# Gate products of the recurrent unit as pairs of 64-row matmuls, one block of 64 channels on each half of the array

## The chip, the core and the metric

The kernel runs on one core of a Trainium2 chip. TensorE multiplies, VectorE (DVE) and ScalarE (ACT) do elementwise work, GpSimd (POOL) keeps small edge columns and issues adding transfers, and SyncE (SP) issues the other transfers. The metric is the device time of one execution in microseconds; the time of a version is the median of its runs.

## What is computed

A decoder layer on 2048 positions of 1024 channels: norm, input projection `w_in`, two mixers side by side, output projection, norm, gated feed-forward with convolutions, norm. The change concerns one mixer, a recurrent unit with 16 heads of 64 channels, whose two gates use one 64x64 matrix per head:

```python
xh = x.reshape(bsz, s, LRU_HEADS, LRU_HEAD_DIM)
r = jax.nn.sigmoid(jnp.einsum('bshi,hij->bshj', xh, wa).reshape(bsz, s, c) + ba)
i = jax.nn.sigmoid(jnp.einsum('bshi,hij->bshj', xh, wx).reshape(bsz, s, c) + bx)
log_a = -RG_C * r * jax.nn.softplus(-lam)
a = jnp.exp(log_a)
b = jnp.sqrt(-jnp.expm1(2.0 * log_a)) * (i * x)
h[t] = a[t] * h[t-1] + b[t]            # then y = h * gelu(gate)
```

`x` here is the convolved projection (the kernel's `cv`), and y goes on to the output projection.

## The kernel before

Channels lie on the 128 partitions, positions along the free dimension, in two halves of 1024 positions, each as two blocks of 512. [...]

For each half of the positions, `in_phase` goes over twelve units in the order L0 L1 S0 L2 L3 S1 L4 L5 S2 L6 L7 S3. An L unit is a block of 128 channels, two heads, of the recurrent mixer; an S unit is one of the short convolution. An input product (`in_product`, 48 matmuls into two PSUM tiles) makes each unit's operands. For an L unit `lru_conv` scales the product out of PSUM (DVE, `evac`, L371), convolves (ACT and DVE, `cv`) and splits the result into `xch` and `xcl`. `gate_weights` splits the block's gate weights into `gw`. `lru_gates` then makes the two gate products: the weights of each gate are a 128x128 matrix with the two heads' 64x64 matrices on the diagonal and zeros elsewhere, and 2 gates x 3 parts x 2 position blocks are 12 matmuls into four PSUM tiles, `zr` and `zi`. They run through `product_step` (L234), the line of the input products too. `lru_scan` follows: sigmoids (ACT, L335), exponential `a`, tanh, square, square root (L342), the scan (DVE, L346) and the multiplication by gelu (L350), which gives y. [...]

After the twelve units come the sweeps of the output projection, a seven-product scheme on blocks of positions and channels. Every sweep has three steps; each step loads a weight page and an activation page (`wr_o`) and splits both (`wh_o`, `fh_o` on ACT, `wl_o`, `fl_o` on DVE). The activation pages are y and sums of y, which go through DRAM (`y_d_B`, `y_d_T`): block 7's y is written and read back for the third step of the first sweep.

The order of the work on TensorE, SP and POOL is that of the program text (`manual_schedule`); ACT and DVE are ordered by a scheduler, by its own estimate of durations and by priorities (`tc.high_priority`: the sigmoids and the evacuations above the weight splits, these above the rest). Each engine then works strictly in its order. PSUM has eight tiles of 512 columns, taken in turn; weights have two raw buffers (`wr`) and ten pages. The gate weights lie in the raw buffer of the input block that is loaded with them, so that buffer is not free before `gw` has been split.

The last lines of the file lay out the inputs on the host, `w_gate` among them.

Of the kernel before, what the change touches and what calls it, by code (L numbers as in the profile page):

```python
# [9 lines left out]
AF = mybir.ActivationFunctionType  # L10
ALU = mybir.AluOpType

P = 128
# [3 lines left out]
T = 1024  # L17
NB = 512
NH = S // T
NLRU = 8  # L20
# [5 lines left out]
HW = 90  # L26
HE = 30
WARM = 11
NOUT = NLRU + NSC
NI = NFF // 2  # L30
NO = NOUT // 2
W_OPS = ["W21", "W11", "W22", "W12"]
# [27 lines left out]
O_BA = O_LCB + 8  # L60
O_BX = O_BA + 8
# [7 lines left out]
def block_kernel(  # L69
# [11 lines left out]
    nc = tc.nc  # L81
# [7 lines left out]
    prm = cp.tile([P, NPAR], F32, name="prm")  # L89
# [24 lines left out]
    def col(o):  # L114
        return prm[:, o : o + 1]
# [4 lines left out]
    def act(name):  # L120
        return page(name, "act", 28)

    def wpage(name):
        return page(name, "w", 10)
# [7 lines left out]
    def raw_tile(name):  # L132
        return sb.tile([P, 6, NB], F32, name=name, tag="wr", bufs=2)

    def pst(name):
        return pp.tile([P, NB], F32, name=name, tag="ps")

    def pst2(name):
        return [pst(f"{name}_b{b}") for b in range(T // NB)]

    def flat(t):
        return t.rearrange("p a b -> p (a b)")

    def r32(ap):
        return ap.bitcast(F32R)

    def blk(b):
        return slice(b * NB, (b + 1) * NB)
# [45 lines left out]
    def split(hi, lo, src):  # L194
        nc.scalar.activation(r32(hi), src, AF.Copy)  # L195
        nc.vector.tensor_tensor(r32(lo), src, hi, ALU.subtract)  # L196
# [6 lines left out]
    gate_raw = {}  # L203

    def load_parts(src, name, parts, gate=None):
        tile_ = raw_tile(f"wr_{name}")
        raw = flat(tile_)
        hi = flat(wpage(f"wh_{name}"))
        lo = flat(wpage(f"wl_{name}"))
        n = T // parts  # L210
        for i in range(parts):
            ks = slice(i * n, (i + 1) * n)
            nc.sync.dma_start(raw[:, ks], src[:, ks])
            with tc.high_priority(offset=HW):
                split(hi[:, ks], lo[:, ks], raw[:, ks])
            if gate is not None and i == 0:
                gate_raw[gate] = tile_[:, 4, : 2 * P]
                nc.sync.dma_start(gate_raw[gate], w_gate[gate])
            yield hi, lo

# [5 lines left out]
    def wcol(hl, k):  # L226
        s = slice(k * P, (k + 1) * P)
        return hl[0][:, s], hl[1][:, s]

    def product_step(ps, w, x, first, last):  # L230
        (whi, wlo), (xhi, xlo) = w, x
        for i, (a, b) in enumerate(((whi, xhi), (whi, xlo), (wlo, xhi))):
            for t in range(T // NB):
                nc.tensor.matmul(  # L234
                    ps[t], r32(a), r32(b[:, blk(t)]), start=(first and i == 0), stop=(last and i == 2)
                )
# [76 lines left out]
    def gate_weights(c, half):  # L313
        raw = gate_raw[c]
        gw = flat(act(f"gw{half}_{c}"))
        hi, lo = gw[:, 0 : 2 * P], gw[:, 2 * P : 4 * P]
        with tc.high_priority(offset=HW):
            split(hi, lo, raw)
        return hi, lo

    def lru_gates(c, half, xc, gw):
        pss = []
        for g, name in enumerate("ri"):
            ps = pst2(f"z{name}{half}_{c}")
            product_step(ps, wcol(gw, g), xc, True, True)
            pss.append(ps)
        return pss

    def lru_scan(c, half, cv, g, ps_r, ps_i):
        n = f"{half}_{c}"  # L330
        r, i, a = (flat(act(f"{x}{n}")) for x in "ria")
        with tc.high_priority(offset=HP):
            for dst, ps, o in ((r, ps_r, O_BA), (i, ps_i, O_BX)):
                for b, p in enumerate(ps):
                    nc.scalar.activation(dst[:, blk(b)], p, AF.Sigmoid, bias=col(o + c))  # L335
        nc.vector.tensor_tensor(i, i, cv, ALU.mult)
        m = cv
        nc.scalar.activation(a, r, AF.Exp, scale=nc8[:, c : c + 1])
        nc.scalar.activation(m, r, AF.Tanh, scale=c8[:, c : c + 1])
        nc.scalar.activation(r, a, AF.Square)  # L340
        nc.vector.scalar_tensor_tensor(m, r, 1.0, m, ALU.add, ALU.mult)
        nc.scalar.activation(m, m, AF.Sqrt)  # L342
        nc.vector.tensor_tensor(i, i, m, ALU.mult)
        h = r
        init = 0.0 if half == 0 else h_last[:, c : c + 1]
        nc.vector.tensor_tensor_scan(h, a, i, init, ALU.mult, ALU.add)  # L346
        if half < NH - 1:
            nc.gpsimd.tensor_copy(h_last[:, c : c + 1], h[:, T - 1 : T])
        nc.scalar.activation(g, g, AF.Gelu_apprx_tanh)
        nc.vector.tensor_tensor(h, g, h, ALU.mult)  # L350
        return h
# [60 lines left out]
    def in_phase(half, acts, acc, between):  # L412
# [29 lines left out]
        for n, (kind, c) in enumerate(UNITS):  # L442
# [22 lines left out]
            if n % 2 == 0:  # L465
                put(y_d[half], 5 if n < NOUT - 2 else 4, n // 2, "B11", y[:, blk(0)])
                even = y
# [7 lines left out]
    def put(dst, when, i, op, src):  # L475
        defer(when, dst[op][i // 2][:, i % 2, :], src)
# [265 lines left out]
    warm = pst("warm")  # L742
    for i in range(WARM):
        nc.tensor.matmul(warm[:, :P], ones, ones, start=True, stop=True)
# [172 lines left out]
def _cols(a):  # L917
    import numpy as np

    a = np.asarray(a)  # L920
    return a.reshape(-1, P).T
# [18 lines left out]
def _arrange(i):  # L940
    import numpy as np

    f = {k: np.asarray(v) for k, v in i.items()}
    x = f["x"]
    out = {}
    out["xT"] = x[0].T.reshape(KC, P, S)
    out["w_in"] = f["w_in"][0].reshape(KC, P, 28, P).transpose(2, 1, 0, 3).reshape(28, P, D)
    wg = np.zeros((NLRU, P, 2, P), x.dtype)
    for g, name in enumerate(("lru_wa", "lru_wx")):
        w = f[name][0].reshape(NLRU, 2, 64, 64)  # L950
        wg[:, 0:64, g, 0:64] = w[:, 0]
        wg[:, 64:128, g, 64:128] = w[:, 1]
    out["w_gate"] = wg.reshape(NLRU, P, 2 * P)
    w = f["w_out"][0].reshape(NOUT, P, D)
    out["w_out"] = _blocks(w[[c if kind == "L" else NLRU + c for kind, c in UNITS]], NO)
    out["w_down"] = _blocks(f["w_down"][0], NI)
    out["w_up"] = f["w_up"][0].reshape(KC, P, 2 * NFF, P).transpose(2, 1, 0, 3).reshape(2 * NFF, P, D)
    out["par"] = np.concatenate(
        [
            _cols(f["norm1_g"][0]),  # L960
            _cols(f["norm2_g"][0]),
            _cols(f["final_g"]),
            _taps(f["lru_conv_w"][0]),
            _cols(f["lru_conv_b"][0]),
            _cols(f["lru_ba"][0]),
            _cols(f["lru_bx"][0]),
            _cols(f["lru_lambda"][0]),
            _taps(f["sc_conv_w"][0]),
            _taps(f["ffn_conv_w"][0]),
        ],  # L970
        axis=1,
    )
    return {k: np.ascontiguousarray(v) for k, v in out.items()}
# [23 lines left out]
```

## Time and profile before

| | us |
|---|---|
| median of 3 runs (2310.92 to 2312.91) | 2312.73 |
| profiled execution | 2314.18 |
| its span, first to last instruction | 2312.4 |
| TensorE busy | 2278.3 |
| DVE busy | 1724.5 |
| ACT busy | 1135.9 |
| granted TensorE clock, mean | 0.993 |

The profile records one execution. A row of a timeline gives start, duration, engine, line, operation, output and inputs, shape and count, and in brackets the engine's idle time before it and what ended that. PEld rows are weight loads, SPq rows are transfers being issued. The chain of waits is followed back from the last instruction. In half 0 the twelve units take from the start to about 345 us, in half 1 from about 490 to 797 us, and the sweeps of the output projection follow each.

### The profile page before, as it was taken

Reading aid. Unit: us, or ns where it says so; the run is one execution under the profiler, and the core shown is the slowest. Engines: PE = TensorE matmul, PEld = TensorE weight load, DVE = VectorE, ACT = ScalarE, POOL = GpSimd, SP = SyncE. Lnnn points to the kernel's source line nnn. Section 1 sums busy time; section 2 is a strip of 40 time slices with the busy share of each in tenths; the row PEclk is TensorE's granted clock in tenths of the full one; section 3 lists DMA queues with packets and bytes.
Section 4 is the critical chain, followed back from the end, with each engine's and each line's share of the span. In section 5 each row is a group of like instructions: output and inputs, shape, how many; then the busy total and the mean of one; then the engine's idle time right before and its main releaser. Section 6 shows DMA issues by size and latency. Waiting matters only on the chain.

```text
span 2312.4 us, 26025 instructions
## 1 busy us (share of the span) xinstructions
PE 2278.3 (99%) x9984; PEld 1879.7 (81%) x9984; DVE 1724.5 (75%) x1910; ACT 1135.9 (49%) x1242; POOL 143.7 (6%) x232
## 2 busy tenths in 40 slices
PE   9999998999999999999999999999999999999997
PEld 7788887888888877888888888888888888888885
DVE  7656667867655799888787877678788887876656
ACT  5553554545543645554444444445544444443443
POOL 0011000001011000011111100000010100000000
PEclk9999999999999999999999999999999999999998
DMA  5356238766666477223232338576223232349754
GB/s 181 108 151 160 69 108 300 265 189 141 187 158 177 158 278 269 98 98 109 97 114 92 114 128 300 190 264 220 87 91 114 91 114 91 114 171 319 262 187 181
DMA packets 145598, 378.29 MB, mean 164 GB/s; under 512 B 13824, under 2 KB 17024, under 8 KB 144896
## 3 DMA queue, kind: packets, MB, share of 16 engines
q1 hardware_dynamic: 135680, 357.74, 44.5%
q0 software_dynamic: 9792, 18.88, 5.1%
q8 instruction: 78, 1.28, 0.2%
q14 instruction: 48, 0.39, 0.1%
HBM read 289.53 MB, written 124.78 MB: 179 GB/s over the span
## 4 chain that ended last, share of the span: by engine, by line
PE 86%; DVE 5%; DMA 5%; ACT 3%; issue 1%; SPq 0%; POOL 0%; DVEq 0%; ACTq 0%; POOLq 0%
PE zx L580 23%; PE zin_b L234 20%; PE zc L580 11%; PE dx L696 11%; PE dy L696 8%; PE za L580 6%; PE ox L696 3%; PE oy L696 3%; DMA wr_in<-in_w_in 1%; DMA wr_o<-y_d_B 1%; PE zr_b L234 1%; PE zi_b L234 1%; DMA x<-in_xT 1%; DMA wr_d<-sd_d_S 0%; DVE fl_o L196 0%
## 5 line engine op out<-in xcount | busy, mean ns | idle before, releaser
L234 PE MATMUL zin_b<-xh,wh_in 128*128 128x512 f32 x896 | 277.8, 391 | 4.3 <-DVE ss_a L270 2.6
L234 PE MATMUL zin_b<-xl,wh_in 128*128 128x512 f32 x896 | 277.2, 391 | 0.2 <-DVE xl L402 0.2
L234 PE MATMUL zin_b<-xh,wl_in 128*128 128x512 f32 x896 | 277.2, 391 | 0.0
L234 PEld LDWEIGHTS zin_b<-xh,wh_in 128*128 128x128 f32 x896 | 169.1, 189 | 40.9 <-DVE ss_a L270 3.4
L234 PEld LDWEIGHTS zin_b<-xl,wh_in 128*128 128x128 f32 x896 | 168.5, 188 | 36.2 <-DVE xl L402 1.5
L234 PEld LDWEIGHTS zin_b<-xh,wl_in 128*128 128x128 f32 x896 | 168.9, 188 | 35.1
L196 DVE TENSOR_TENSOR fl_d<-wr_d,fh_d 128x1024 fp32r<-128x1024 f32 x84 | 102.7, 1222 | 94.1 <-ACT fh_d L195 91.7
L195 ACT ACTIVATE fh_d<-wr_d 128x1024 fp32r<-128x1024 f32 x84 | 89.1, 1061 | 170.2 <-PE dx L696 84.2
L196 DVE TENSOR_TENSOR wla_up<-wr_up,wha_up 128x1024 fp32r<-128x1024 f32 x48 | 58.8, 1225 | 143.2 <-ACT wha_up L195 143.2
L195 ACT ACTIVATE wh_in<-wr_in 128x1024 fp32r<-128x1024 f32 (+1 forms) x62 | 60.2, 974 | 191.1 <-DMA wr_in<-in_w_in 174.3
L696 PE MATMUL dx<-fl_d,wh_d 128*128 128x512 f32 x384 | 149.6, 389 | 0.8 <-DVE fl_d L196 0.8
L696 PE MATMUL dx<-fh_d,wl_d 128*128 128x512 f32 x384 | 149.4, 389 | 0.0
L696 PE MATMUL dx<-fh_d,wh_d 128*128 128x512 f32 x384 | 149.4, 389 | 0.0
L196 DVE TENSOR_TENSOR wl_in<-wr_in,wh_in 128x1024 fp32r<-128x1024 f32 (+1 forms) x62 | 69.1, 1119 | 106.2 <-ACT wh_in L195 106.2
L556 DVE TENSOR_TENSOR wr_up<-wr_up 128x512 f32<-128x512 f32 x192 | 129.8, 685 | 7.6 <-DMA wr_up<-in_w_up 6.4
L196 DVE TENSOR_TENSOR wl_d<-wr_d,wh_d 128x1024 fp32r<-128x1024 f32 x84 | 102.5, 1220 | 39.5 <-ACT wh_d L195 37.1
L580 PE MATMUL zc<-hhB,whd_up 128*128 128x512 f32 x384 | 126.0, 389 | 0.0
L294 DVE SCALAR_TENSOR_TENSOR cu<-un,prm,cu 128x1024 f32<-128x1024 f32 x96 | 122.5, 1277 | 4.3 <-ACT cu L290 4.3
L294 DVE SCALAR_TENSOR_TENSOR cg<-ug,prm,cg 128x1024 f32<-128x1024 f32 x96 | 122.7, 1278 | 0.4
L195 ACT ACTIVATE wh_d<-wr_d 128x1024 fp32r<-128x1024 f32 x84 | 88.5, 1053 | 67.5 <-DMA wr_d<-sd_d_S 39.0
L580 PE MATMUL zx<-ht,whc_up 128*128 128x512 f32 x384 | 118.2, 389 | 0.0
L591 ACT ACTIVATE ug<-zx 128x512 f32<-128x512 f32 x96 | 57.5, 599 | 122.6 <-PE zx L580 122.6
(257 smaller groups left out, 5599.7 us busy)
## 6 DMA issues: line engine op xcount, KB each, us to landing
wr_up<-in_w_up SPq DMA_DIRECT2D x96, 512.0 KB, 4.8
wr_in<-in_w_in SPq DMA_DIRECT2D x54, 512.0 KB, 4.2
wr_d<-sd_d_S SPq DMA_DIRECT2D x48, 512.0 KB, 3.8
wr_d<-f_d_T SPq DMA_DIRECT2D x48, 512.0 KB, 5.2
f_d_B<-cu SPq DMA_DIRECT2D x72, 256.0 KB, 2.4
wr_d<-in_w_down SPq DMA_DIRECT2D x36, 512.0 KB, 3.6
wr_d<-f_d_B SPq DMA_DIRECT2D x36, 512.0 KB, 4.6
wr_o<-so_d_S SPq DMA_DIRECT2D x24, 512.0 KB, 4.5
```

The lines of the kernel that those rows point to most:

```text
L195: nc.scalar.activation(r32(hi), src, AF.Copy)
L196: nc.vector.tensor_tensor(r32(lo), src, hi, ALU.subtract)
L234: nc.tensor.matmul(ps[t], r32(a), r32(b[:, blk(t)]), start=(first and i == 0), stop=(last and i == 2))
L294: nc.vector.scalar_tensor_tensor(dst, src[:, k : k + T], col(o_w + k), dst, ALU.mult, ALU.add)
L556: nc.vector.tensor_tensor(raw[:, o, :], raw[:, a, :], raw[:, b, :], ALU.add)
L580: nc.tensor.matmul(ps, r32(p[:, s]), r32(self.hs[k][x][o]), start=f and i == 0, stop=l and i == 2, skip_group_check=True,)
L591: nc.scalar.activation(dst, self.x, AF.Copy)
L696: nc.tensor.matmul(ps[m], r32(p), r32(x[:, k, :]), start=first and i == 0 and n == 0, stop=(last or not on_x) and i == ni - 1 and n == 2, ...
```

## The change

Each gate product becomes two matmuls of 64 rows, one per head, that use the upper and the lower half of the array's rows. The weights of a block are now 128x128 for both gates together, without zeros: the rows of the first head hold its r matrix, then its i matrix, the rows of the second head its i matrix, then its r matrix. So the first PSUM tile (still called zr in the listings) holds r of the first head on partitions 0 to 63 and i of the first head on 64 to 127, and the other tile (zi) i and r of the second head. The sigmoids then take 64 partitions each, those of i crossing from one half of the partitions to the other. Gate weights, their transfer and their splits have half the columns.

```diff
-                gate_raw[gate] = tile_[:, 4, : 2 * P]
+                gate_raw[gate] = tile_[:, 4, :P]
...
-        hi, lo = gw[:, 0 : 2 * P], gw[:, 2 * P : 4 * P]
+        hi, lo = gw[:, :P], gw[:, P : 2 * P]
...
     def lru_gates(c, half, xc, gw):
-        pss = []
-        for g, name in enumerate("ri"):
-            ps = pst2(f"z{name}{half}_{c}")
-            product_step(ps, wcol(gw, g), xc, True, True)
-            pss.append(ps)
+        pss = [pst2(f"z{name}{half}_{c}") for name in "ri"]
+        for i, (a, b) in enumerate(((gw[0], xc[0]), (gw[0], xc[1]), (gw[1], xc[0]))):
+            for t in range(T // NB):
+                for ps, rows in zip(pss, HALVES):
+                    nc.tensor.matmul(ps[t], r32(a[rows, :]), r32(b[rows, blk(t)]), start=i == 0, stop=i == 2)
         return pss
...
-            for dst, ps, o in ((r, ps_r, O_BA), (i, ps_i, O_BX)):
-                for b, p in enumerate(ps):
-                    nc.scalar.activation(dst[:, blk(b)], p, AF.Sigmoid, bias=col(o + c))
+            for dst, o, order in ((r, O_BA, (0, 1)), (i, O_BX, (1, 0))):
+                for rows, ps, k in zip(HALVES, (ps_a, ps_b), order):
+                    for b, p in enumerate(ps):
+                        nc.scalar.activation(
+                            dst[rows, blk(b)], p[HALVES[k], :], AF.Sigmoid, bias=prm[rows, o + c : o + c + 1]
+                        )
...
-    wg = np.zeros((NLRU, P, 2, P), x.dtype)
-    for g, name in enumerate(("lru_wa", "lru_wx")):
-        w = f[name][0].reshape(NLRU, 2, 64, 64)
-        wg[:, 0:64, g, 0:64] = w[:, 0]
-        wg[:, 64:128, g, 64:128] = w[:, 1]
-    out["w_gate"] = wg.reshape(NLRU, P, 2 * P)
+    w = [f[name][0].reshape(NLRU, 2, 64, 64) for name in ("lru_wa", "lru_wx")]
+    out["w_gate"] = np.concatenate(
+        [np.concatenate([w[k][:, k], w[1 - k][:, k]], axis=2) for k in range(2)], axis=1
+    )
```

The sigmoids' number moves ACT's order in other places too. First, the start of half 0 on ACT, before: `rh_a`, `ry_a` belong to the mean of squares, `wh_in` with 9, 20, 24 and 16 are splits of input weight blocks, `cv_0` the convolution of block 0.

```order
L195 ACTIVATE rh_a_476<-ss_a_271 128x1024
L195 ACTIVATE wh_in_9_606<-wr_in_9_605 128x1024
L195 ACTIVATE wh_in_20_715<-wr_in_20_714 128x1024
L269 ACT_TABLE_LOAD
L269 ACTIVATE ry_a_545<-ms_a_0_539,eps 128x512
L269 ACTIVATE ry_a_545<-ms_a_512_540,eps 128x512
L195 ACTIVATE wh_in_24_818<-wr_in_24_817 128x1024
L292 ACTIVATE cv_0_558<-xl_0_553,prm 128x1024
```

The same place in the changed kernel:

```order
L196 ACTIVATE rh_a_476<-ss_a_271 128x1024
L196 ACTIVATE wh_in_9_606<-wr_in_9_605 128x1024
L196 ACTIVATE wh_in_20_719<-wr_in_20_718 128x1024
L196 ACTIVATE wh_in_24_826<-wr_in_24_825 128x1024
L270 ACT_TABLE_LOAD
L270 ACTIVATE ry_a_545<-ms_a_0_539,eps 128x512
L270 ACTIVATE ry_a_545<-ms_a_512_540,eps 128x512
L196 ACTIVATE wh_in_16_890<-wr_in_16_889 128x1024
```

The split of block 24 has moved ahead of the root of the mean, and that of block 16 ahead of the convolution. In the same way the split of block 10 has moved from behind `xch` of block 1 to ahead of the convolution of block 1.

Second, ACT at the end of half 0, from the gelu of block 7 to the first sweep's second step, before; `cv_6` and `cv_7` are here the square roots, `r_7` and `i_7` the sigmoids.

```order
L349 ACTIVATE g_7_2347<-g_7_2347 128x1024
L342 ACT_TABLE_LOAD
L342 ACTIVATE cv_6_2102<-cv_6_2102 128x1024
L195 ACTIVATE wh_o_0_0_2594<-wr_o_0_0_2585 128x1024
L195 ACTIVATE fh_o_0_0_2598<-wr_o_0_0_2585 128x1024
...
L340 ACTIVATE r_7_2425<-a_7_2427 128x1024
L342 ACT_TABLE_LOAD
L342 ACTIVATE cv_7_2257<-cv_7_2257 128x1024
L195 ACTIVATE wh_o_0_1_2630<-wr_o_0_1_2626 128x1024
```

And in the changed kernel:

```order
L353 ACTIVATE g_7_2375<-g_7_2375 128x1024
L344 ACTIVATE r_6_2290<-a_6_2292 128x1024
L196 ACTIVATE wh_o_0_0_2626<-wr_o_0_0_2617 128x1024
L196 ACTIVATE fh_o_0_0_2630<-wr_o_0_0_2617 128x1024
L346 ACT_TABLE_LOAD
L346 ACTIVATE cv_6_2126<-cv_6_2126 128x1024
...
L344 ACTIVATE r_7_2453<-a_7_2455 128x1024
L196 ACTIVATE wh_o_0_1_2662<-wr_o_0_1_2658 128x1024
L346 ACT_TABLE_LOAD
L346 ACTIVATE cv_7_2281<-cv_7_2281 128x1024
```

Both square roots now stand behind sweep splits that they stood ahead of, and the square of block 6 behind the gelu of block 7. Half 1 shows the same exchange. The orders of SP and POOL have not moved, and on TensorE only the 12 matmuls of each gate stage have changed places among themselves.

More of the change, by code (lines that the diff above doesn't have):

```diff
@@ L28 @@
 WARM = 11
+HALVES = (slice(0, P // 2), slice(P // 2, P))
 NOUT = NLRU + NSC
@@ L321, in lru_gates, with lru_scan @@
     def lru_gates(c, half, xc, gw):
-        pss = []
-        for g, name in enumerate("ri"):
-            ps = pst2(f"z{name}{half}_{c}")
-            product_step(ps, wcol(gw, g), xc, True, True)
-            pss.append(ps)
+        pss = [pst2(f"z{name}{half}_{c}") for name in "ri"]
[3 more added lines that the diff above has]
+                    nc.tensor.matmul(ps[t], r32(a[rows, :]), r32(b[rows, blk(t)]), start=i == 0, stop=i == 2)
         return pss
-    def lru_scan(c, half, cv, g, ps_r, ps_i):
+    def lru_scan(c, half, cv, g, ps_a, ps_b):
         n = f"{half}_{c}"
```

## The prediction

> **What bounds the kernel now.** I read the page first, then the gate tile, then the chain and the timelines around the places where TensorE stands still.
>
> ```profile
> span 2312.4 us, 26025 instructions
> PE 2278.3 (99%) x9984; PEld 1879.7 (81%) x9984; DVE 1724.5 (75%) x1910; ACT 1135.9 (49%) x1242; POOL 143.7 (6%) x232
> PE 86%; DVE 5%; DMA 5%; ACT 3%; issue 1%; SPq 0%; POOL 0%; DVEq 0%; ACTq 0%; POOLq 0%
> ```
>
> TensorE is busy nearly all the time and is 86% of the chain of waits, so matmul time taken out of a stretch without stalls shortens the span. The next view is the gate tile: its matmuls, their weight loads, and the sigmoid that reads it.
>
> ```profile
> L234 PE MATMUL zr_b<-xch,gw x64: 389/389/501, 60.0 to 773.7; 128*128 128x512 f32 x64
> L234 PEld LDWEIGHTS zr_b<-xch,gw x64: 186/188/189, 60.0 to 773.4; 128*128 128x128 f32 x64
> L335 ACT ACTIVATE r<-zr_b,prm x32: 677/686/692, 70.7 to 775.3; 128x512 f32<-128x512 f32 x32
> ```
>
> A matmul is on record with 389 ns, but what counts is the step from one to the next. The chain from 133 us shows it for two gate stages (channel blocks 2 and 3).
>
> ```profile
> 133.36 1.36 PE zr_b L234 x6
> 134.72 1.36 PE zi_b L234 x6
> 136.08 21.76 PE zin_b L234 x96
> 157.84 1.36 PE zr_b L234 x6
> ```
>
> Six matmuls take 1.36 us, 96 take 21.76: 0.227 us each. A gate stage is 12 matmuls, 2.72 us, and there are 16 (eight blocks in each half): 43.5 us in all. Half of that, 21.8 us, is the most that pairs can give.
>
> **The pair on TensorE.** The change keeps 12 matmuls per stage, as six pairs, and each still streams 512 columns. If the two of a pair run at once, a stage is 6 x 0.227 = 1.36 us, plus the lag of the second behind the first. That lag is the spacing of two weight loads, which a stage that had waited shows:
>
> ```profile
> 59.95 0.30 PEld L234 LDWEIGHTS zr_b<-xch,gw 128*128 128x128 f32 x2 [0.52 <-ACT xch L195]
> ```
>
> Two loads end 0.30 us after the first began and one is 0.19, so they start 0.11 apart. Two loads per pair need 0.22 us, just under the 0.227 of a pair: they fit, barely. So a stage is 1.47 us. New as well is the change of array shape ahead of and behind each stage. No row shows one; it costs between nothing and one matmul's undrained rest (0.389 - 0.227 = 0.16) plus a load that cannot be fetched ahead (0.11), 0.27 us. I take half, 0.135, twice per stage: 1.74 us, a saving of 0.98 us (0.71 to 1.25) per stage. The Trainium skill (TensorEngine Tiling (Array Packing), section Tiling Modes) says that changing the tiling mode drains TensorE; no run here shows it, and by it I would take 0.71 and the sum below would be 2.7 us worse for the ten free stages.
>
> **The sigmoids.** Each stage now has eight sigmoids of 64 partitions in place of four of 128. ACT's rows around gate 1:
>
> ```profile
> 67.23 1.06 ACT L195 ACTIVATE xch<-cv 128x1024 fp32r<-128x1024 f32 x1 [2.72 <-DVE cv L294]
> 70.70 1.27 ACT L335 ACTIVATE r<-zr_b,prm 128x512 f32<-128x512 f32 x2
> 71.86 1.27 ACT L335 ACTIVATE i<-zi_b,prm 128x512 f32<-128x512 f32 x2
> 74.44 1.15 ACT L338 ACTIVATE a<-r,nc 128x1024 f32<-128x1024 f32 x1
> 75.50 0.40 ACT L195 ACTIVATE gw<-wr_in 128x256 fp32r<-128x256 f32 x1
> ```
>
> A copy of 1024 columns takes 1.06 us and one of 256 takes 0.40, so ACT's time goes by columns, and a 64x512 sigmoid has the columns of the old one. Its bounds are half the old price (no time added) and the whole; I take the whole, since the row with as many columns is the nearest. Sigmoids start 0.58 us apart (two from 70.70, the next at 71.86), so a stage adds 4 x 0.58 = 2.3 us to ACT, 37 us in all. ACT is half idle, so the total is covered; what matters is what is queued behind them in order.
>
> **The start of half 0.** TensorE stands still here for the mean of squares and for gates 0 and 1.
>
> ```profile
> 44.33 1.28 ACT L269 ACT_TABLE_LOAD   x1 [4.57 <-PE ms_a L265]
> 45.62 1.26 ACT L269 ACTIVATE ry_a<-ms_a,eps 128x512 f32<-128x512 f32 x2
> 41.04 0.33 SPq L213 DMA_DIRECT2D wr_in<-in_w_in  x1
> 50.05 0.33 SPq L213 DMA_DIRECT2D wr_in<-in_w_in  x1
> 53.67 1.04 ACT L195 ACTIVATE wh_in<-wr_in 128x1024 fp32r<-128x1024 f32 x1
> 58.84 1.06 ACT L195 ACTIVATE xch<-cv 128x1024 fp32r<-128x1024 f32 x1 [4.13 <-DVE cv L294]
> ```
>
> The new ACT order has the split of weight block 24 ahead of the table load and root. That block is requested at 41.04; the next one, requested at 50.05, was split at 53.67, 3.6 us later. So the split runs from 44.65, the table load follows at 45.6 and the root at 46.9: 1.3 us late. The split of block 16 (its buffer free at 47.0, then 3.6 for the load, 1.1 on ACT and 1.2 on DVE: 52.9) stands ahead of the first evacuation on DVE, and xch of block 0 comes 1.5 us late. That eats the saving of gate 0: of its stage, 4 pairs follow the late operand where 10 matmuls did, and TensorE leaves it 0.35 us later than before. Gate 1 then waits for its weights, the gw of 75.50 above, behind block 0's sigmoids. xch of block 1 (67.23) moves to about 69.05, since the split of block 10, which stood between it and the sigmoids, is now ahead of it. From there: table load to 71.4, eight sigmoids to 76.15, table load to 77.45, exponential, gw to 78.8, 2.9 us later than the 75.9 of before. TensorE, 0.35 us late itself, then waits 4 us instead of 1.5. What a wait of that length does, the windows show (busy us of PE, PEld, DVE, ACT and POOL, then granted clock, DMA share, GB/s):
>
> ```profile
> 44.40:47.10 2.70, 0.06 (x2) 0.01 (x1) 0.76 (x2) 2.69 (x4) 0.00 (x0) 0.97 0.00 0
> 47.10:50.50 3.40, 3.40 (x8) 2.53 (x9) 3.37 (x4) 0.73 (x1) 0.00 (x0) 0.52 0.00 0
> 74.20:76.00 1.80, 0.48 (x3) 0.06 (x2) 0.26 (x2) 1.79 (x4) 0.00 (x0) 1.00 0.00 0
> 76.00:80.00 4.00, 4.00 (x18) 3.31 (x19) 0.35 (x1) 3.95 (x4) 0.00 (x0) 1.00 0.00 0
> ```
>
> After 2.7 us idle the granted clock was 0.52 for 3.4 us, a loss of 1.6; after the 1.5 us at gate 1 it stayed at 1.00. A wait of 4 us should lose 1.7. Gate 1: 2.9 late, 1.1 shorter, 1.7 lost: **+3.5 us** after it (+1.0 without the clock's drop and with a quicker load, to +4.5).
>
> **The ten free stages** (gates 2 to 5, and 0 to 5 of half 1) wait for nothing in the trace. The closest is the second of a pair of blocks:
>
> ```profile
> 147.94 1.27 ACT L335 ACTIVATE r<-zr_b,prm 128x512 f32<-128x512 f32 x2
> 153.77 0.40 ACT L195 ACTIVATE gw<-wr_in 128x256 fp32r<-128x256 f32 x1
> ```
>
> Eight sigmoids end at 152.7 there; table load, exponential, then gw, now ahead of the tanh: ready at 155.4, where TensorE arrives at 157.84 - 0.98 = 156.9. So 10 x 0.98 = **-9.8 us** (-7.1 to -12.5).
>
> **Gates 6 and 7 and the change to the sweeps.** After them the sweep's third step needs block 7's y through DRAM, and its sixth stalls TensorE.
>
> ```profile
> 308.54 1.27 ACT L335 ACTIVATE i<-zi_b,prm 128x512 f32<-128x512 f32 x2
> 318.25 1.06 ACT L342 ACTIVATE cv<-cv 128x1024 f32<-128x1024 f32 x1
> 319.21 1.05 ACT L195 ACTIVATE wh_o<-wr_o 128x1024 fp32r<-128x1024 f32 x1
> 325.10 1.23 DVE L350 TENSOR_TENSOR r<-g,r 128x1024 f32<-128x1024 f32 x1
> 330.17 0.58 SPq L707 DMA_DIRECT2D wr_o<-in_w_out  x1
> 334.30 1.06 ACT L342 ACTIVATE cv<-cv 128x1024 f32<-128x1024 f32 x1
> 335.27 1.04 ACT L195 ACTIVATE wh_o<-wr_o 128x1024 fp32r<-128x1024 f32 x1
> 341.21 1.25 DVE L350 TENSOR_TENSOR r<-g,r 128x1024 f32<-128x1024 f32 x1
> 342.52 0.32 SPq L192 DMA_DIRECT2D y_d_B<-r  x1
> 362.00:372.00 10.00, 10.00 (x46) 8.29 (x45) 3.79 (x5) 1.06 (x1) 0.00 (x0) 1.00 1.05 390
> 377.34 0.49 PE L696 MATMUL oy<-fh_o,wh_o 128*128 128x512 f32 x1 [4.62 <-ACT fh_o L195]
> ```
>
> Block 6's sigmoids end 2.3 us later; its square root (318.25) also falls behind two sweep splits (1.9 us): 4.2 late. DVE does its two splits meanwhile, so y of block 6 (325.10) is 1.8 late. SP holds the next sweep load (330.17) behind the writes of that y, so the load is 1.8 late too and lands near 337.1; its split now stands ahead of block 7's square root, which moves from 334.30 to about 339.3. With multiply, split and scan behind it y of block 7 (341.21) starts 3.7 us late. The write at 342.52 waits for it, all loads behind that write too, and to the stall's end the DMA engines run full (share 1.05), so nothing is caught up: the exit at 377 is 3.7 us later, and the 2 x 0.98 us of gates 6 and 7 are spent waiting. Half 1 has the same order there and I take the same. Together **+7.4 us** (from -3.9, if the delay is hidden and all four stages count, to +9).
>
> **Sum.** 3.5 - 9.8 + 7.4 = +1.1 us on the span of 2312.4. That execution took 2314.18, 1.45 over the median of 2312.73; on the median it gives **2314 us** (2313.8). Smaller gate loads and splits (0.1 us each on ACT and DVE) lie beside idle time and count nothing.
>
> **Rivals.** (1) The sigmoids' time is absorbed: half-width ones cost half, or ACT's half-idle time swallows them. Then y of blocks 6 and 7 is not late: 1.0 - 9.8 - 3.9 = -12.7, 2300 us. For it: ACT is busy 49% of the span. Against: the rows by columns, and this stretch, which holds the sigmoids of blocks 6 and 7 and in which ACT is busy 23.17 of 23.40 us:
>
> ```profile
> 304.00:327.40 23.40, 23.40 (x105) 19.39 (x104) 14.77 (x15) 23.17 (x25) 1.03 (x1) 1.00 0.17 57
> ```
>
> (2) The two halves don't overlap, so the change doesn't do what it says. A stage costs 0.27 more, not less: start 2.9 + 0.27 + 1.7 = +4.9, ten stages +2.7, the two ends +7.4: +15.0, 2328 us. Every matmul of the trace uses the whole array, so no row excludes it. (3) Slower by weight loads: a load waits until its own half is done, a pair takes 0.227 + 0.11 = 0.334, a stage 2.38 with its switches, and the saving is 0.34, 0.64 less per stage: 3.5 + 0.6 - 3.4 + 7.4 = +8.1, 2321 us. It decides if loads cannot run under their own half's matmul. The trace speaks against it: loads are busy 81% beside matmuls at 99%. The Trainium skill (TensorE: Matmul & The Clock Gate, Part 3: Packing small matmuls) says that loads overlap matmuls under way only where the row group differs, which is this rival; for full-array matmuls the trace disagrees, with those same 81%.
>
> **Chances.** Forecast 0.48, rival 1 0.24, rival 2 0.12, rival 3 0.16. The range, 2300 to 2326, takes in rival 3 and the upper half of rival 1 and stops short of rival 2; the forecast's own is 2307 to 2319. A measurement tells about 0.2%, 4.6 us, from no change. Of the forecast I count 0.12 as faster, 0.60 same, 0.28 slower; rival 1 faster, rival 2 slower, rival 3 0.3 same and 0.7 slower: faster 0.30, same 0.34, slower 0.36.
>
> **What would show it.** In the new profile: starts of the two matmuls of a pair about 0.11 us apart and pairs 0.23 (else rival 2 or 3); from the last ordinary matmul to the next ordinary one 1.5 to 2.0 us where nothing is waited for; sigmoids of 64x512 at 0.69 us; gate 1 waiting some 4 us for gw with a clock near 0.5 after it; stalls of the first sweeps longer by about 5 us in each half, now also in the third step. Wrong I would be first if y of block 7 is no later, or if a shape change costs more than 0.27 us.

## The result and the profile after

| | before | after |
|---|---|---|
| median of 5 runs each, us | 2312.91 | 2328.96 |
| lowest and highest, us | 2310.92, 2313.64 | 2324.68, 2331.53 |
| span of the profiled execution, us | 2312.4 | 2329.8 |
| granted TensorE clock, mean | 0.993 | 0.987 |

The ratio is 1.0068 with a 95% interval from 1.0055 to 1.0081: the change costs 16 us. The forecast of 2314 us was too low, and the range, which ended at 2326, did not hold the time. First the page of the changed kernel: span, busy time, and the chain of waits by engine and by line.

```profile
span 2329.8 us, 26115 instructions
PE 2274.3 (98%) x9984; PEld 1864.1 (80%) x9984; DVE 1723.2 (74%) x1910; ACT 1177.3 (51%) x1307; POOL 141.6 (6%) x232
PE 61%; DMA 10%; DVE 9%; ACT 7%; issue 2%; SPq 0%; DVEq 0%; ACTq 0%; POOL 0%; POOLq 0%
PE zx L584 22%; PE zc L584 11%; PE dx L700 9%; PE dy L700 6%; PE za L584 6%; DMA wr_in<-in_w_in 4%; PE zin_b L235 2%; PE oy L700 2%; PE ox L700 2%; ACT wh_in L196 1%; DVE cv L295 1%; DVE wl_in L197 1%; ACT i L337 1%; DMA wr_d<-f_d_T 1%; DVE
```

TensorE's share of the chain fell from 86% to 61%, while its busy time hardly moved. The input products (`zin_b`) are on it with 2% only: through most of the twelve units the time is now set by weight loads, ACT and DVE. These two split every operand: `split` writes a high part with a copy on ACT and a low part with a subtraction on DVE, and a product is high x high, high x low and low x high. ACT is busy 41 us longer (1177.3 against 1135.9), a little more than the 37 of the forecast.

**The gate stage itself does what it should.** The timeline of block 2's gates in half 0, where nothing is waited for (rows in between left out):

```profile
136.16 0.18 PEld L327 LDWEIGHTS zr_b<-xch,gw 64*128 64x128 f32 x1 [0.35 <-issue]
136.16 0.49 PE L327 MATMUL zr_b<-xch,gw 64*128 64x512 f32 x1
136.17 0.18 PEld L327 LDWEIGHTS zi_b<-xch,gw 64*128 64x128 f32 x1
136.17 0.50 PE L327 MATMUL zi_b<-xch,gw 64*128 64x512 f32 x1
136.27 0.19 PEld L327 LDWEIGHTS zr_b<-xch,gw 64*128 64x128 f32 x1
...
136.50 0.39 PE L327 MATMUL zr_b<-xch,gw 64*128 64x512 f32 x1
136.50 0.18 PEld L327 LDWEIGHTS zr_b<-xcl,gw 64*128 64x128 f32 x1
136.51 0.38 PE L327 MATMUL zi_b<-xch,gw 64*128 64x512 f32 x1
136.51 0.41 PEld L327 LDWEIGHTS zi_b<-xcl,gw 64*128 64x128 f32 x2
...
137.75 0.50 PE L235 MATMUL zin_b<-xh,wh_in 128*128 128x512 f32 x1
```

The two matmuls of a pair start 0.01 us or less apart, and so do their weight loads: the halves of the array load side by side. From the first pair to the next input product it is 1.59 us (136.16 to 137.75), where twelve matmuls took 2.72. The first pair comes 0.09 us later than an ordinary matmul would, and the first input matmuls behind the pairs lose 0.12 more. So a free stage gives 0.91 us, as the step from one gate stage to the next shows: 23.57 us from gate 2 to gate 3 of half 0 (136.16 to 159.73), 24.48 before (133.20 to 157.68).

**Where the time went.** The table follows TensorE through the program; its rows are starts of matmuls in the two timelines. The forecast's column adds up its own terms (+3.5, 0.98 per free stage, 3.7 at the end of each half).

| TensorE starts | after less before, us | forecast, us |
|---|---|---|
| gate 2 of half 0 (136.16, 133.20) | +3.0 | +3.5 |
| gate 6 of half 0 (295.87, 296.40) | -0.5 | -0.4 |
| gate 0 of half 1 (519.31, 513.22) | +6.1 | +3.3 |
| gate 6 of half 1 (749.94, 748.05) | +1.9 | -2.6 |
| last step of the first sweeps of half 1 (926.96, 911.55) | +15.4 | +1.1 |
| end of the span | +17.4 | +1.1 |

Up to gate 6 of half 0 the forecast holds to 0.5 us. The two ends lose 6.6 and 13.5 us where it had 3.7 each. The timeline of TensorE shows the stalls there, in half 0 and in half 1; the brackets hold the idle time and what ended it. Before, each half had one large stall (5.0 and 3.0 us from matmul to matmul); now each has two, the first at a new place, the third step of the first sweep, and in half 1 gate 7 waits too.

```profile
353.57 0.39 PE L700 MATMUL ox<-fh_o,wl_o 128*128 128x512 f32 x1
360.96 0.80 PE L700 MATMUL ox<-fh_o,wh_o 128*128 128x512 f32 x1 [7.00 <-ACT fh_o L196]
...
383.56 0.76 PE L700 MATMUL oy<-fh_o,wh_o 128*128 128x512 f32 x1 [2.94 <-ACT fh_o L196]
385.45 0.80 PE L700 MATMUL oy<-fl_o,wh_o 128*128 128x512 f32 x1 [1.13 <-DVE fl_o L197]
...
776.64 0.79 PE L327 MATMUL zr_b<-xch,gw 64*128 64x512 f32 x1 [3.06 <-ACT gw L196]
...
819.28 0.80 PE L700 MATMUL ox<-fh_o,wh_o 128*128 128x512 f32 x1 [6.80 <-ACT fh_o L196]
...
840.66 0.51 PE L700 MATMUL oy<-fh_o,wh_o 128*128 128x512 f32 x1 [2.15 <-ACT fh_o L196]
841.92 0.80 PE L700 MATMUL oy<-fl_o,wh_o 128*128 128x512 f32 x1 [0.75 <-DVE fl_o L197]
```

Part of the loss is the clock behind the stalls: from 345 to 395 us TensorE is busy 38.5 us at a mean granted clock of 0.83 (before 44.0 at 0.93), from 800 to 850 us 39.9 at 0.86 (before 46.6 at 0.97).

The scan of block 7, on which the first stall of each end depends, starts 8.3 us later than before in half 0 (346.04, before 337.74) and 15.2 later in half 1 (805.05, before 789.84). So ACT and DVE fell behind TensorE, more in half 1, long before gate 6. The table has, in us after less before, the start of the gate stage on TensorE and the start of the multiplication that gives y on DVE, for four blocks of each half:

| | half 0: 1 | 3 | 5 | 7 | half 1: 1 | 3 | 5 | 7 |
|---|---|---|---|---|---|---|---|---|
| gate | +1.3 | +2.1 | +0.3 | -1.4 | +5.5 | +3.7 | +1.9 | +4.1 |
| y | +2.2 | +7.4 | +3.5 | +7.5 | +10.9 | +8.7 | +11.5 | +14.2 |

TensorE catches up from gate to gate; y does so only in part in half 0 and hardly in half 1, where 8.7 us at block 3 are 11.5 again at block 5. Half 1 begins with block 0's y 12.3 us late: gate 0 is 6.1 late, and ACT has the sigmoids of blocks 0 and 1, eight more than before at 0.63 us each, ahead of block 0's root. What keeps y from catching up, the chain of waits shows in half 1 (start, duration, engine and work; short pieces left out):

```profile
617.59 2.36 DVE r L350
619.97 1.24 DVE r L354
...
624.47 0.49 SPq L193
...
625.00 0.64 SPq L360
...
625.74 6.49 DMA wr_in<-in_w_in
...
632.25 1.07 ACT wh_in L196
633.35 1.22 DVE wl_in L197
634.57 2.27 DVE r L350
636.87 1.24 DVE r L354
...
638.17 0.33 SPq L193
...
639.46 8.74 DMA wr_in<-in_w_in
```

Scan and y of block 2 (L350, L354), then SP's writes of it (L193), behind them the next weight load; its split on ACT and DVE, ahead of the scan of block 3 in DVE's order; y of block 3, SP's write of it, and the next load behind that. It is a loop: **y late, write late, load late, split late, next y late.** TensorE is nowhere in it. Before, the same two loads were issued at 617.94 and 631.70: the loop is now 7.8 us behind, while TensorE is 3.7 behind at gate 3. SP's own waits for y in the twelve units of half 1 (490 to 800 us) rise from 127 to 140 us: us in all, times, longest; first the kernel before, then the changed one.

```profile
SPq L192 <- DVE yc L482: 65.2, 4, 19.9
SPq L192 <- DVE r L350: 61.6, 4, 30.8
```

```profile
SPq L193 <- DVE r L354: 73.0, 4, 36.9
SPq L193 <- DVE yc L486: 67.2, 4, 22.3
```

### The profile page after: what moved, and what is told of

Read it like the earlier page. It is cut to its first block, busy times and chain, and to the rows that moved or that the text cites. A ratio compares the mean times of both kernels' runs of the same rounds, so it can differ in the third digit from the quotient of the medians.

```text
span 2329.8 us, 26115 instructions
## 1 busy us (share of the span) xinstructions
PE 2274.3 (98%) x9984; PEld 1864.1 (80%) x9984; DVE 1723.2 (74%) x1910; ACT 1177.3 (51%) x1307; POOL 141.6 (6%) x232
## 3 DMA queue, kind: packets, MB, share of 16 engines
q8 instruction: 78, 1.28, 0.2%
## 4 chain that ended last, share of the span: by engine, by line
PE 61%; DMA 10%; DVE 9%; ACT 7%; issue 2%; SPq 0%; DVEq 0%; ACTq 0%; POOL 0%; POOLq 0%
PE zx L584 22%; PE zc L584 11%; PE dx L700 9%; PE dy L700 6%; PE za L584 6%; DMA wr_in<-in_w_in 4%; PE zin_b L235 2%; PE oy L700 2%; PE ox L700 2%; ACT wh_in L196 1%; DVE cv L295 1%; DVE wl_in L197 1%; ACT i L337 1%; DMA wr_d<-f_d_T 1%; DVE r L350 1%
```

## The experiments

All times are medians against runs of the kernel before on the same chip (2312.6 to 2314.7 us), and ratios carry their 95% intervals. A difference of 2 to 3 us between two versions is within their scatter.

**Each half of the change alone.** First the eight sigmoids on before's matmuls:

```diff
-                for b, p in enumerate(ps):
-                    nc.scalar.activation(dst[:, blk(b)], p, AF.Sigmoid, bias=col(o + c))
+                for rows in HALVES:
+                    for b, p in enumerate(ps):
+                        nc.scalar.activation(
+                            dst[rows, blk(b)], p[rows, :], AF.Sigmoid, bias=prm[rows, o + c : o + c + 1]
```

> The 128-row matmuls and gate weights of before, with eight sigmoids of 64 partitions in place of four of 128: the second half of the change alone. Theory A (ACT's longer stretch of sigmoids lengthens a loop from ACT over the weight loads and the writes of y back to ACT, and the ends of the two halves pay for it): all of the change's loss is here, 2324 to 2332 us, with the sixth steps of the first sweeps left 5 us or more later than before in half 0 and 10 or more in half 1. Rival B (the loss is TensorE's own: shape changes and a lower clock around the pairs): no loss here, 2311 to 2316 us.

Then the pairs with four sigmoids:

```diff
-            for dst, o, order in ((r, O_BA, (0, 1)), (i, O_BX, (1, 0))):
-                for rows, ps, k in zip(HALVES, (ps_a, ps_b), order):
...
+            for dst, ps, o in ((r, ps_a, O_BA), (i, ps_b, O_BX)):
+                for b, p in enumerate(ps):
+                    nc.scalar.activation(dst[:, blk(b)], p, AF.Sigmoid, bias=col(o + c))
```

> The pairs of 64-row matmuls with four sigmoids of 128 partitions, as before: r is taken from the first PSUM tile and i from the second, so the halves of the two heads' r and i are not exchanged and half of the gate values are the other gate's; all amounts of work but the four further sigmoids of a stage are those of the changed kernel. Theory A: TensorE's 1.04 us per stage is kept, by 12 to 16 stages: 2296 to 2302 us. Rival B: 2313 us or more, as in the changed kernel.

Measured: eight sigmoids alone 2334.53 us (1.0094, 1.0076 to 1.0112), pairs alone 2318.42 us (1.0021, 1.0012 to 1.0031). The first is 2.5 us above theory A's range, and far from rival B. The second fell to rival B's number, but not for its reason: its gate stages are as short as those above. TensorE is 4.3 us ahead of the kernel before at gate 4 of half 0 and 1.5 behind at gate 5, where it waits for gate weights; the two ends take most of the rest. ACT in that run, from the square of block 3 to its square root, then TensorE at gate 5:

```profile
168.74 1.06 ACT L341 ACTIVATE r<-a 128x1024 f32<-128x1024 f32 x1
177.85 1.06 ACT L196 ACTIVATE wh_in<-wr_in 128x1024 fp32r<-128x1024 f32 x1 [8.04 <-DMA wr_in<-in_w_in]
178.92 1.28 ACT L343 ACT_TABLE_LOAD   x1
180.22 1.06 ACT L343 ACTIVATE cv<-cv 128x1024 f32<-128x1024 f32 x1
```

```profile
240.77 0.79 PE L327 MATMUL zr_b<-xch,gw 64*128 64x512 f32 x1 [5.91 <-ACT gw L196]
```

ACT stands 8.04 us before a weight load, with block 3's root behind it in its order. y of block 3 is late by that, SP's next load by y: the loop again, with no instruction added. In the kernel before, this root stood ahead of the split (174.02 and 180.20); the gate stages with their weights are all that is shorter here, so they made the scheduler turn the two round. A faster TensorE alone was worth less than nothing.

**What holds the loads?** Two candidates: the raw buffer that is not free until `gw` has been split, and SP, which waits for y with the load behind it. Gate weights split early (in the text right behind their load):

```diff
                     cur = (*cur, lru_gate(c, half, in_product(NLRU + c, half, acts), rs))
+                    gw = gate_weights(c, half)
...
                 ps_n = ps_2 or in_product(first_product(nxt), half, acts)
...
-                if n > 0:
-                    gw = gate_weights(c, half)
```

> The changed kernel with the split of a block's gate weights moved in the program text from behind the next unit's input product to right behind the load that brings them, so that it is not queued behind the sigmoids of the block before, and the raw buffer is freed earlier. Theory A1 (the raw buffer that is held until gw is split closes the loop): the wait of gate 1 in half 0 goes (6 us with the clock's drop and the 1.5 us it had before), that of gate 7 in half 1 too (3 to 5), and sweeps begin earlier: 2311 to 2319 us. Theory A2 (the loop runs over the writes of y, behind which SP holds the loads): gate 1 gains, but the ends of the halves give most of it back: 2321 to 2327 us.

Three raw buffers (in this and the next of its kind the pool is exchanged ahead of the feed-forward part):

```diff
-        return sb.tile([P, 6, NB], F32, name=name, tag="wr", bufs=2)
+        if raw_pool[0] is not None:
+            return raw_pool[1].tile([P, 4, NB], F32, name=name, tag="wr", bufs=3)
+        return raw_pool[1].tile([P, 6, NB], F32, name=name, tag="wr", bufs=2)
```

> The changed kernel with three raw weight buffers of four pages in place of two of six up to the end of the second half's sweeps (the same space; six pages are used in the feed-forward part alone). Theory A1 (a raw buffer held until gw is split makes the loads wait): one buffer is always left, loads start 4 to 8 us earlier in the second half, splits no longer keep the sigmoids behind them in ACT's queue: 2314 to 2321 us. Theory A2 (SP holds the loads behind late writes of y): 2326 to 2331 us, as the changed kernel.

Early splits gave 2329.93 us (1.0076, 1.0062 to 1.0091), nothing, which neither theory had: gate 1 no longer waits, but gate 3 then waits 4.4 us for its weights, and the ends stall as before. Three buffers gave 2318.16 us (1.0018, 1.0009 to 1.0027), 11 us less than the changed kernel, which seemed to speak for the buffer. The same on the kernel before:

> The kernel before with three raw weight buffers of four pages, as the control of the run that gave them to the changed kernel (11 us faster than the changed one). Theory L (before, the loop of loads, splits, sigmoids and writes of y just keeps up with TensorE, and the change pushes it over): only the ends of the halves can gain, 2305 to 2311 us. Rival G (a third buffer is worth as much to any kernel of this shape and says nothing of the change): the same 11 us, 2302 us or less.

It came to 2315.09 us (1.0009, 1.0000 to 1.0018), above both theories: no gain; the exchange of pools costs TensorE some 5 to 8 us in these runs (idle time and the halved clock behind it, estimated from their profiles), which hides what the ends of the halves gain. So the third buffer is not good in general; it helps where the loop is closed. The other candidate, the writes of y, put into SP's order two loads later:

```diff
-                put(y_d[half], 5 if n < NOUT - 2 else 4, n // 2, "B11", y[:, blk(0)])
+                put(y_d[half], 7 if n < NOUT - 2 else 4, n // 2, "B11", y[:, blk(0)])
...
-                combine(y_d[half], 5, n // 2, even, y, c, d)
+                combine(y_d[half], 7 if n < NOUT - 2 else 5, n // 2, even, y, c, d)
```

> The changed kernel with two raw buffers, but the writes of y for the first ten units are put into SP's order seven loads after their unit instead of five, so that a late y holds fewer loads back. Theory A1 (it is the raw buffer that is not free): 2326 to 2331 us, as the changed kernel. Theory A2 (it is SP that waits for y with the next load behind it): 2316 to 2323 us.

2313.02 us (1.0003, 0.9994 to 1.0012): **one number in SP's order, at two places, takes the whole 16 us back**, more than theory A2 asked for. SP's waits for y in half 1's units, 140 us in the changed kernel, fall to 43:

```profile
SPq L193 <- DVE r L354: 35.4, 2, 27.9
SPq L193 <- DVE yc L486: 7.3, 1, 7.3
SPq L214 <- DVE gw L197: 111.3, 6, 29.7
SPq L214 <- DVE wl_in L197: 65.8, 16, 21.7
```

The last two rows are waits for a raw buffer, which is free when the splits have read it. They are 177 us here and 97 in the changed kernel (67.0 and 29.7), so SP waits about as long in all as it did. The sum of its waits therefore says little; what counts is which wait has a load behind it that TensorE will miss. And y now catches up: in half 1 it is 11.5 us late at block 3, 2.1 at block 5 and 0.3 at block 7.

Two controls on the kernel before, later writes and, the other way, writes three loads after their unit:

> The kernel before with the writes of y seven loads later, as the control of the run that gave this to the changed kernel (16 us off it). Theory L (before, SP's waits for y just stay hidden behind TensorE; the change uncovers them): only the ends of the halves can gain, 2307 to 2313 us. Rival G (later writes are worth as much to any kernel of this shape): 2297 to 2302 us.

> The kernel before with the writes of y for the first ten units three loads after their unit instead of five; nothing of the change is in it, no instruction is added. If SP's wait for y, with weight loads queued behind it, is what makes the loop: the kernel before falls into it as well, 2320 to 2335 us. If the changed kernel's loss needs its own sigmoids or order: 2311 to 2316 us.

Later writes gave before 2316.71 us (1.0011, 1.0002 to 1.0020): no gain, rather 2 us lost, which neither theory had. In its profile gate 1 of half 0 waits 2.2 us for `gw`, before 1.3, and behind it the granted clock is halved for 3.4 us, which it was not before; gate 2 is 2.9 us late by that. Why `gw` comes later there stays open. Sooner writes gave 2339.75 us (1.0109, 1.0096 to 1.0123): **the kernel before falls into the loop without anything of the change in it**, deeper than the changed kernel and 5 us beyond the range expected. SP's waits for y in half 0's units (60 to 345 us) are 179 us there, 132 in the kernel before (69.6 and 62.3), and TensorE stands before input weights, which it never did:

```profile
SPq L192 <- DVE r L350: 92.2, 3, 44.7
SPq L192 <- DVE yc L482: 86.4, 4, 30.4
```

```profile
PE zin_b L234 <- ACT wh_in L195: 8.7, 3, 5.2
```

The longest of these waits can be followed in the rows of that run: the last write of y, the load behind it, its split, TensorE.

```profile
171.69 1.32 SPq L192 DMA_DIRECT2D y_d_T<-yd  x1
173.80 0.68 SPq L213 DMA_DIRECT2D wr_in<-in_w_in  x1
182.40 1.06 ACT L195 ACTIVATE wh_in<-wr_in 128x1024 fp32r<-128x1024 f32 x1 [7.43 <-DMA wr_in<-in_w_in]
183.51 1.11 PE L234 MATMUL zin_b<-xh,wh_in 128*128 128x512 f32 x2 [5.16 <-ACT wh_in L195]
```

In these runs the scheduler also moved some 20 of ACT's 1240 to 1310 rows and 35 to 50 of DVE's 1910; with sooner writes block 3's root is among them, as with pairs alone. That root stands behind the split of 182.40 and cannot have held it. So that the place of the writes decides is shown; that the moved rows do nothing is read from such chains and was not tested by itself.

**The two halves of the change with the loop opened:**

> Pairs with four sigmoids of 128 partitions (the exchange of halves between r and i left out) and the writes of y seven loads later, two raw buffers. Theory L: with the loop opened most of TensorE's 16 us come through: 2296 to 2303 us. Rival O (with pairs alone ACT's order, moved by the shorter matmuls, is the loss of 2318 us): 2310 to 2320 us.

> Before's matmuls with eight sigmoids of 64 partitions and the writes of y seven loads later. Theory L (most of the 21 us that the eight sigmoids cost alone is the loop over SP, the rest the waits of gate 1 and of the sweeps for y of block 7): 2316 to 2324 us. Rival S (the sigmoids cost by themselves, whoever waits for y): 2330 to 2335 us.

Pairs with four sigmoids 2301.99 us (0.9947, 0.9935 to 0.9960), as theory L has it; eight sigmoids on before's matmuls 2326.47 us (1.0053, 1.0040 to 1.0067), outside what either theory said. With this the change can be taken apart; pairs alone leaves out the exchange of r and i, so it shows a time and not a kernel to use. Differences from the kernel before, as ratios times 2313 us:

| writes of y after | unchanged | pairs alone | eight sigmoids alone | both |
|---|---|---|---|---|
| five loads | 0 | +5 | +22 | +16 |
| seven loads | +3 | -12 | +12 | +1 |

With seven loads the parts add up to within the scatter: pairs take 15 us (16 stages of 0.91 make 14.6), with eight sigmoids 11 to 12; the sigmoids cost 10 to 13. With five they don't: pairs lose 5 or gain 6, and sigmoids cost 22 or 11, as it comes.

**Several edits together.** Pairs with four sigmoids and three buffers; the changed kernel with three buffers, early splits and later writes; with early splits and later writes:

> Pairs with four sigmoids of 128 partitions (the exchange of halves between r and i left out, as in the run before with two buffers: 2318 us), now with three raw buffers. Theory L (pairs alone lost because weight loads, which no longer hid behind a slower TensorE, could not come earlier): 16 us of TensorE's time come through, 2293 to 2303 us. Rival O (it is ACT's order, moved by the shorter matmuls, that made pairs alone lose): 2312 to 2320 us.

> The changed kernel with three things at once: three raw buffers, gate weights split right behind their load, writes of y seven loads later. If buffers, the place of gw and SP's waits are separate causes, it gains what each gave and the 6 us of gate 1: 2305 to 2313 us. If the third buffer has taken all there is, as with it alone: 2316 to 2320 us.

> The changed kernel with the writes of y seven loads later and the gate weights split right behind their load, two raw buffers. If gate 1's wait (4.5 us and a lower clock behind it, 7 in all) is now the largest stall that a split in time removes: 2305 to 2309 us. If, as with early splits alone, later gates then wait for gw instead: 2311 to 2315 us.

2307.00 us (0.9979, 0.9969 to 0.9989), 2311.28 us (0.9996, 0.9987 to 1.0004) and 2314.55 us (1.0003, 0.9994 to 1.0012). The first lies between its theories; some 8 us of it stand at the exchange of pools (4.7 us idle from 907 us on, the rest the halved clock), so without them it would be near 2299, as theory L had it; that is an estimate. The second lies in its first range, but within the scatter of later writes alone, so the gains of its three edits don't add up. The third says that gate weights split early for all blocks give nothing beyond later writes.

**ACT's time per stage.** Not every change of function on ACT costs a table load: in the kernel before, the tanh of 170.46 follows the exponential of 165.86 with no ACT_TABLE_LOAD row between them, while the sigmoids have a load of 1.28 us ahead of them. So a sigmoid written as 0.5 + 0.5 tanh(z/2) takes about one load off each stage:

```diff
-                            dst[rows, blk(b)], p[HALVES[k], :], AF.Sigmoid, bias=prm[rows, o + c : o + c + 1]
+                            dst[rows, blk(b)], p[HALVES[k], :], AF.Tanh, scale=0.5, bias=hb[o][rows, c : c + 1]
...
-        nc.vector.tensor_tensor(i, i, cv, ALU.mult)
+        nc.vector.scalar_tensor_tensor(i, i, 1.0, cv, ALU.add, ALU.mult)
...
-        nc.scalar.activation(m, m, AF.Sqrt)
+        nc.scalar.activation(m, m, AF.Sqrt, scale=0.25)
```

> The changed kernel with the tanh form alone, writes of y where they were. If ACT's time per stage goes round the closed loop (2.65 us per stage cost 21 us without pairs and 11 with them there): 2317 to 2324 us. If the loop is SP's wait whatever ACT does: 2327 to 2331 us.

> The changed kernel with the writes of y seven loads later and the sigmoids written as 0.5 + 0.5 tanh(z/2): the half goes into the scale and bias of the exponential and the tanh behind it, the one into VectorE's product, the last half into the square root's scale. Tanh needs no table of its own beside the exponential's, so 16 of ACT's 70 table loads go, 1.28 us per stage. If ACT's time per stage has a price with the loop opened (eight sigmoids, 2.65 us per stage, cost some 10 us there): about 5 us less than with later writes alone, 2305 to 2310 us. If only the place of y's writes counts: 2311 to 2315 us.

> The kernel before with the same two edits, as control. TensorE sets its pace outside the start and the ends of the halves, so the 1.28 us per stage can be had at gate 1 and at the ends alone: 2310 to 2315 us, at most 4 us less than with later writes alone (2316.7 us).

On the changed kernel alone 2322.30 us (1.0036, 1.0022 to 1.0050), 7 us less for 20 us of ACT (busy 1157.3 against 1177.3; 57 table loads, not 74); with later writes 2310.10 us (0.9984, 0.9976 to 0.9993), 3 to 4 less than without the tanh form, at the end of what was expected; on the kernel before with both 2311.79 us (0.9990, 0.9981 to 0.9999), 5 less than with later writes alone, where 4 at most were expected. So about a third of what is taken off ACT's stages comes back in the closed loop, a sixth to a quarter in the open one.

**The fastest complete version** adds the early split for block 1 alone, whose gate still waited 2.9 us in half 0:

```diff
                     ps_g = in_product(NLRU + nxt[1], half, acts)
+                    gw_1 = gate_weights(nxt[1], half)
...
-                    gw = gate_weights(c, half)
+                    gw = gw_1 if n == 1 else gate_weights(c, half)
```

> The changed kernel with later writes of y and the tanh form (2310.1 us), and in each half the gate weights of block 1 alone split right behind their load. If gate 1's wait of 3.0 us in half 0 is paid in full: 2306 to 2308 us. If the end of the half gives it back, as its last steps wait for block 7's y through DRAM: 2309 to 2311 us.

> The kernel before with later writes of y, the tanh form and the gate weights of block 1 split right behind their load: the control of the fastest version (2306.8 us). Gate 1 no longer waits in the kernel before with the first two edits (2311.8 us), so nothing more is to be had there: 2310 to 2313 us, and the change itself is worth 4 to 6 us in these surroundings. If it comes to 2307 us as well, the change is worth nothing there.

2306.79 us (0.9976, 0.9967 to 0.9986): 6 us faster than the kernel before and 22 faster than the changed one. The kernel before with the same three edits comes to 2311.18 us (0.9988, 0.9979 to 0.9997). In these surroundings the change is worth 3 us by the ratios (4 by the medians), and the two intervals overlap: that it gains at all is not shown.

## Why the prediction was wrong

**The pair on TensorE**: right. The stage gives 0.91 us (forecast 0.98, from 0.71 to 1.25). The pair is closer than taken: the loads of its halves run side by side (136.16 and 136.17), so the lag of 0.11 does not exist. The change of shape costs more: 0.09 us ahead of the first pair, and in the rows above 0.34 from the first pair to the second (136.16 to 136.50) where 0.23 is the pace, 0.32 from the last pair (137.43) to the input product and 0.12 more behind it, some 0.45 per stage against 0.27. The two errors nearly cancel. The Trainium skill (TensorEngine Tiling (Array Packing), section Tiling Modes) says that a change of mode drains TensorE; the trace agrees that it costs, and puts some 0.2 us on each.

**Rival 2** (no overlap) falls with the same rows, although its 2328 us happens to lie beside the result: 12 matmuls in sequence would need 2.72 us and more for what took 1.59. **Rival 3** falls too. Weight loads run while their own half multiplies: the load of 136.27 lies within the matmul of 136.16 to 136.65 on the same rows. The Trainium skill's rule for it (TensorE: Matmul & The Clock Gate, Part 3: Packing small matmuls), that loads overlap only with matmuls of other rows, is not what this trace shows, for half the array as for the whole.

**The sigmoids**: right. 64 partitions cost what 128 do:

```profile
L337 ACT ACTIVATE r<-zr_b,prm x32: 668/678/689, 69.4 to 787.1; 64x512 f32<-64x512 f32 x32
```

Eight start 0.63 us apart and take 5.1 us where four took 2.4, 2.7 more per stage (forecast 2.3). **Rival 1** falls as far as it said that this is absorbed; what it saw is that their time decides: without it and with the loop opened the pairs reach 2302 us, beside its 2300.

**The start of half 0**: right in size, +3.0 against +3.5, but by two errors that cancel. The split of block 24, now ahead of the root, began at 42.38 and was done before the mean of squares was, so the mean's stall did not grow. `gw` of block 1 was ready at 77.15, 1.25 us later than before, where 2.9 was forecast. TensorE came to the gate earlier, and so still waited the 4 us of the forecast; behind that the granted clock was 0.50 for 5.9 us and not for 3.4, which lost some 2.6 us (forecast 1.7). The sum is 1.3 late, 0.9 shorter, 2.6 lost (windows as in the prediction; behind the five engines comes the granted clock):

```profile
77.20 0.79 PE L327 MATMUL zr_b<-xch,gw 64*128 64x512 f32 x1 [4.01 <-ACT gw L196]
```

```profile
72.90:77.30 4.40, 0.39 (x4) 0.10 (x2) 1.34 (x2) 4.36 (x7) 0.00 (x0) 0.90 0.00 0
77.30:83.20 5.90, 5.90 (x19) 4.20 (x20) 1.40 (x2) 5.84 (x6) 0.00 (x0) 0.50 0.00 0
```

**The ten free stages**: TensorE ran ahead as forecast in half 0 (3.5 us over four stages) and by 4.2 us over six in half 1, where small waits, for `gw` and for a sigmoid among them, took some of it: -7.7 against -9.8. But this was not yet a gain of the program, since the chain behind did not follow.

**The step that failed is "Gates 6 and 7 and the change to the sweeps"**: +7.4 forecast, 20 measured (6.6 and 13.5). It was worked out from the lateness of blocks 6 and 7 alone, 2.3 us of sigmoids and 1.9 of moved order, as if y of all blocks before them were on time; and it took half 1 to be like half 0. The part that it worked out is about right: from block 5 to block 7 y gets 4.0 us later in half 0 and 2.7 in half 1, where 3.7 was forecast. What it put at nothing, without a reason, is the lateness that y already has at block 5: 3.5 us in half 0 and 11.5 in half 1, while TensorE's gate 5 is 0.3 and 1.9 late. SP holds the next weight loads behind each late write, and so the lateness is handed from block to block instead of being made up. The prediction did see the wait of SP behind y, but only at the end, for block 6; that the same wait stands at every pair of blocks it did not price. Nor did it have a term for the clock behind the longer stalls. What the profile offered for it were SP's waits, 127 to 132 us in each half for y with a load behind them, in a kernel whose TensorE never showed it.

With the loop opened the changed kernel takes 2313.02 us, near the forecast's 2314. In that profile the steps of the table above come to +3.7, -3.6, +3.2, -4.3 and +2.3, where the forecast had +3.5, -3.9, +3.7, -5.9 and +3.7. So its terms were sound to within 1.6 us for a chain with slack, which was not there; that the sum agrees to 1 us is partly luck, since later writes cost the kernel before 2 us.

## What to carry to other kernels

An engine that is busy all the time may hide a second loop that is nearly as long; what a faster stage is worth is then bounded by the loop's slack. Ask of every wait of a queue, hidden or not, what stands behind it, and whether that feeds what it waits for. If the parts of a change don't add up when each is run alone, look for such a loop, and open it (here by one number in the order of the transfers) before the change is judged.

## What was not expected of the hardware

- The two matmuls of a pair on the upper and the lower 64 rows start within 0.01 us of each other, and so do their weight loads of 0.18 us.
- A change between 128-row and 64-row matmuls costs some 0.2 us each way (0.45 per gate stage), spread over the matmuls on both sides of it.
- A matmul's record of 0.39 us stays the same with half the rows, and a sigmoid's of 0.68 us with half the partitions.
